# A hybrid decoder layer: order and number of GpSimd's clears before attention, and products of 128 columns in place of 256

## The chip, the cores and the metric

The kernel runs on one core of a Trainium2 chip. The time is that of one execution on the device, in microseconds; the kernel before takes 741.02 us (median of 3 runs, 740.92 to 741.1). The core has a matrix engine (TensorE, PE in the profile), a vector engine (VectorE, DVE), a scalar engine (ScalarE, ACT), GpSimd (POOL), and SyncE (SP), which here only issues DMA transfers.

## The reference

One decoder layer over 512 tokens of 1024 channels. Two causal attention branches of 8 heads (64 channels a head) work on the same modulated input; their outputs are projected, gated, merged, and followed by a layer norm and a gated MLP with a short causal convolution. The part that the change touches is attention:

```python
logits = einsum('bhqd,bhkd->bhqk', q, k) * ATTN_SCALE + c[..., None] - c[:, :, None, :]
p = softmax(where(kpos <= qpos, logits, -inf))            # forgetting branch
y_fox = einsum('bhqk,bhkd->bhqd', p, v)

z = einsum('bhqd,bhkd->bhqk', q, k) * ATTN_SCALE           # stick-breaking branch
rest = reverse_cumsum(where(kpos < qpos, log_sigmoid(-z), 0)) (exclusive)
a = where(kpos < qpos, exp(log_sigmoid(z) + rest), 0)
y_sb = einsum('bhqk,bhkd->bhqd', a, v)
```

`c` is the running sum of log forget gates. Both branches are causal: a query block of 128 tokens needs only the key blocks up to its own.

## The kernel before, in words

Matrix products are done in a 32-bit type that TensorE reads with fewer mantissa bits (fp32r; the profile prints operands of products as f32). To keep precision, an operand is split into a high and a low part, `hi_of` on ACT (line 91) and `lo_of` on DVE (line 94), and a product is the sum of three: high by high, high by low, low by high. Projections go through `mm3` (lines 132 to 134), 512 columns each.

First comes a stage that loads the modulation weights and does the first projections while loading (line 336). Attention follows. Its work is a list of projections (`stream`, through `proj` and `vgroup`) that fills TensorE between the steps of 16 heads: 8 of the stick-breaking branch (branch 1) first, then 8 of the forgetting branch (branch 0). The head loop calls for each head `stage_a`, `stage_b` and `stage_c`, with `fill(n)` for so many projection products between them. The order of SyncE's DMA issues is that of the source; on the other engines the framework's planner orders the instructions, and may move one ahead of another whose inputs it expects later. So TensorE's instructions do not always lie in the order of the source.

`stage_a` computes the scores of the four query blocks i, in the order 0, 2, 1, 3, by two products each: line 512 with `m1` (key, high part above and once more below), line 513 with `m2`, whose upper 64 rows hold the key's low part (line 455) and whose lower 64 rows are zero in the stick-breaking branch; in the forgetting branch four of them carry the decay terms (`decay_rows`: four rows of ones, then rows of `chi` by GpSimd's DMAs). Block i needs (i + 1) x 128 columns of keys, but no product is narrower than 256 (line 510): block 0 computes 128 columns that nobody reads. The scores lie in three PSUM banks (`OFS`); block 0 has the first 128 columns of bank 0, and block 2 the other 384. In branch 1, ACT takes two sigmoids of each bank (lines 535, 536), DVE scans (540) and GpSimd multiplies (541).

`m2` and its partner on the query side, `s2`, are views of four rotating tiles each (`m2t`, `s2t`). GpSimd clears their lower halves once, before attention: each query tile by three pieces (64 rows to 0, four to 1, two to -1, lines 375 to 377), then each key tile by one (line 379). In branch 1 `s2` is not used; `s1` stands in for it.

`stage_b` transposes the weights block by block on TensorE (line 561, plain fp32 with the identity) and splits them. The third group holds block (3,3), then (2,2) and (2,3), in a tile `ptc` of 512 columns from column 128 on; columns 0 to 127 of `ptc` are zero, cleared once by GpSimd (line 371).

`stage_c` multiplies values by the transposed weights (line 579), for each of the high and low parts one product per key block j, in the order 0 to 3. Key block 3 touches only query block 3, that is 128 columns, but its product takes 256, of which the first 128 are the zeros of `ptc` (`AVL`).

Of the kernel before, what the change touches and what calls it, by code (L numbers as in the profile page):

```python
# [9 lines left out]
F32R = mybir.dt.float32r  # L10
# [6 lines left out]
P = 128  # L17
# [34 lines left out]
def layer_kernel(ctx: ExitStack, tc: tile.TileContext, out, xT, x, c8, wa0, wa1, bcol, w1, wct, wv, bf,  # L52
# [3 lines left out]
    V, S, G, PE = nc.vector, nc.scalar, nc.gpsimd, nc.tensor  # L56
# [16 lines left out]
    def nm(s):  # L73
        cnt[0] += 1
        return f"{s}_{cnt[0]}"

    def bank():
        return pp.tile([P, 512], F32, name=nm("ps"), tag="ps")
# [8 lines left out]
    def fl(ap):  # L87
        return ap.bitcast(F32)

    def hi_of(o, i, scale=1.0):  # L90
        S.activation(o, i, AF.Copy, scale=scale)

    def lo_of(o, i, hi):
        state["read"] = V.tensor_tensor(o, i, fl(hi), ALU.subtract)  # L94
        return state["read"]
# [32 lines left out]
    def z(dt, s, shape=(P, 512)):  # L128
        return zp.tile(list(shape), dt, name=nm(s), tag="z", bufs=NZ)
# [14 lines left out]
    def weights(i, ahead=AHEAD):  # L144
        while state["load"] < min(len(items), i + depth[0]):
            it = items[state["load"]]
            if it[2] == 512:
                late = state.get("late")
                it[3] = late.tile([P, 512], F32, name=nm("rl"), tag="rl", bufs=4) if late else z(F32, "rs")
            else:  # L150
                it[3] = stg.tile([P, 1024], F32, name=nm("raw"), tag="raw", bufs=LOADS)
            c = 0
            for src in it[0] if isinstance(it[0], list) else [it[0]]:
                w = src.shape[-1]
                d = nc.sync.dma_start(it[3][:, c : c + w], src)
                c += w
                if depth[0] < LOADS and state["load"] >= depth[0]:
                    if reads[state["load"] - depth[0]] is None:
                        release()
                    paced(d, reads[state["load"] - depth[0]])  # L160
            if len(it) > 5:
                G.dma_start(it[3], it[5], accum_op=ALU.add)  # L162
            state["load"] += 1
            while state["proc"] <= state["load"] - depth[0]:
                process()
        while state["proc"] < min(len(items), i + 1 + ahead):
            process()
        return items[i][4]
# [42 lines left out]
    for k in range(KT):  # L211
        o = grp[k // 4][:, k % 4 * P : (k % 4 + 1) * P]
# [151 lines left out]
    att = st2.enter_context(tc.tile_pool(name="att", bufs=1, reuse_waits="tile"))  # L364

    OFS = ((0, 0), (2, 0), (0, 128), (1, 0))
    SEG = (((0, 128), (128, 512)), ((0, 512),), ((0, 256),))
    ptc = [[att.tile([P, 512], F32R, name=f"ptc{i}{e}", tag=f"ptc{i}{e}") for e in range(2)] for i in range(2)]
    for e in ptc:
        for t in e:  # L370
            G.memset(fl(t[:, 0:128]), 0.0)
    s2t = [att.tile([P, 512], F32R, name=f"s2_{i}", tag=f"s2_{i}") for i in range(4)]
    m2t = [att.tile([P, 512], F32R, name=f"m2_{i}", tag=f"m2_{i}") for i in range(4)]
    for t in s2t:
        G.memset(fl(t[64:128, :]), 0.0)
        G.memset(fl(t[64:68, :]), 1.0)
        G.memset(fl(t[64:66, :]), -1.0)
    for t in m2t:
        G.memset(fl(t[64:128, :]), 0.0)
    chi = att.tile([NH, 2, 512], F32R, name="chi", tag="chi")  # L380


# [22 lines left out]
    def decay_rows(h):  # L405
        n = slot_free(idx(0, h))
        if h < 4:
            G.memset(fl(m2t[n][64:68, :]), 1.0)
        G.dma_start(s2t[n][66:68, :], chi[h : h + 1, :, :])
        G.dma_start(m2t[n][64:66, :], chi[h : h + 1, :, :])  # L410
# [9 lines left out]
    def idx(br, h):  # L420
        return h if br == 1 else NH + h
# [43 lines left out]
    def v_part(br, h, j):  # L465
        o = ((h // 2) % 2) * 256 + (h % 2) * P
        return vt[(br, j, h // 4)][:, o : o + P]
# [36 lines left out]
    def stage_a(br, h):  # L504
        d = hd[(br, h)]
        bk = [bank(), bank(), bank()]

        def scores(i):
            b, o = OFS[i]
            w = max(256, (i + 1) * P)  # L510
            tb = slice(i * P, (i + 1) * P)
            PE.matmul(bk[b][:, o : o + w], d["s1"][:, tb], d["m1"][:, 0:w], start=True, stop=False)  # L512
            PE.matmul(bk[b][:, o : o + w], d["s2"][:, tb], d["m2"][:, 0:w], start=False, stop=True)  # L513

        for i in (0, 2, 1, 3):
            scores(i)
        pt = [z(F32, "pt"), z(F32, "pt"), z(F32, "pt")]
        if br == 0:
            sm = att.tile([P, 12], F32, name=nm("sm"), tag="sm", bufs=3)
            for i in (0, 2, 1, 3):  # L520
                b, o = OFS[i]
                c = slice(o, o + (i + 1) * P)
                n, m = pt[b][:, c], mska[:, (3 - i) * P : 512]
                V.tensor_tensor_reduce(n, bk[b][:, c], m, -1.0, -NEG, ALU.add, ALU.min, sm[:, i : i + 1])
                S.activation(n, n, AF.Exp, scale=-1.0, bias=sm[:, i : i + 1], accum_out=sm[:, 4 + i : 5 + i])
            V.reciprocal(sm[:, 8:12], sm[:, 4:8])
            for i in (0, 2, 1, 3):
                b, o = OFS[i]
                c = slice(o, o + (i + 1) * P)
                V.tensor_scalar_mul(pt[b][:, c], pt[b][:, c], sm[:, 8 + i : 9 + i])  # L530
        else:
            for b in (0, 2, 1):
                w = SEG[b][-1][1]
                om = z(F32, "om")
                S.activation(om[:, 0:w], bk[b][:, 0:w], AF.Sigmoid, scale=-1.0)  # L535
                d["last"] = S.activation(pt[b][:, 0:w], bk[b][:, 0:w], AF.Sigmoid)
                G.memset(pt[b][:, SEG[b][0][1] - 1 : w : 384], 0.0)
                for s, e in SEG[b]:
                    d0 = om[:, s + 1 : e][:, ::-1]
                    V.tensor_tensor_scan(d0, d0, dg[:, 513 - (e - s) : 512][:, ::-1], 0.0, ALU.mult, ALU.max)  # L540
                    G.tensor_tensor(pt[b][:, s : e - 1], pt[b][:, s : e - 1], om[:, s + 1 : e], ALU.mult)  # L541
        d["pt"] = pt
        scored.add(idx(br, h))
        if br == 0 and h + 4 < NH:
            decay_rows(h + 4)
        if br == 1 and h >= 4 and gated:
            decay_rows(h - 4)
# [3 lines left out]
    def stage_b(br, h):  # L551
        d = hd[(br, h)]
        pt = d["pt"]
        n = h % 2
        d["ph"], d["pl"] = [], []
        for e, lst in enumerate(TRL):
            bk = bank()
            w = len(lst) * P
            for q, (j, i) in enumerate(lst):
                b, o = OFS[i]  # L560
                PE.transpose(bk[:, q * P : (q + 1) * P], pt[b][:, o + j * P : o + (j + 1) * P], ident)  # L561
            if e < 2:
                ph, pl, o = z(F32R, "ph"), z(F32R, "pl"), 0
            else:
                (ph, pl), o = ptc[n], 128
            hi_of(ph[:, o : o + w], bk[:, 0:w])
            lo_of(pl[:, o : o + w], bk[:, 0:w], ph[:, o : o + w])
            d["ph"].append(ph)
            d["pl"].append(pl)

    AVL = ((0, 0, 0, 0, 512), (1, 1, 0, 128, 384), (2, 2, 256, 256, 256), (3, 2, 0, 256, 256))
    yf, yh, yl = {}, {}, {}

    def stage_c(br, h):
        d = hd.pop((br, h))
        ps = bank()
        for a, src in enumerate((d["ph"], d["pl"])):
            for j, e, so, to, w in AVL:
                PE.matmul(ps[:, to : to + w], v_part(br, h, j), src[e][:, so : so + w], start=a == 0 and j == 0, stop=a == 1 and j == 3)  # L579
# [227 lines left out]
    stage_a(1, 1)  # L807
    fill(48)
    stage_b(1, 0)
    fill(48)  # L810
    heads = [(br, 2 * p + e) for br, p in seq for e in range(2)]
# [182 lines left out]
    for n in range(2 * FT):  # L994
# [7 lines left out]
        if n in (23, 27):  # L1002
            t = t13[(23, 27).index(n)][:, 0:512]
# [5 lines left out]
        if n in (28, 31, 32, 35):  # L1009
            k = (28, 31, 32, 35).index(n)  # L1010
            w = wdp[FP - 1][:, k * 512 : (k + 1) * 512]
# [115 lines left out]
    for n in range(2 * FT):  # L1127
# [27 lines left out]
        t = z(F32, "cv")  # L1155
# [131 lines left out]
    for n, k in enumerate(wi):  # L1287
        w = weights(k)
        for a, p in enumerate(range(2 * n, min(FP - LATE, 2 * n + 2))):
            t = ops[p][3]  # L1290
# [5 lines left out]
    for i in range(2):  # L1296
        pieces = [(1, 0, 512)] if i == 0 else [(1, 0, 256), (1, 256, 512)]
        for n, (e, c0, c1) in enumerate(pieces):
            ps = bank()[:, 0 : c1 - c0] if i else W1[0]
            for q in range(LATE):  # L1300
                t = ops[FP - LATE + q][3]
# [72 lines left out]
```

## Time and profile before

| | |
|---|---|
| median of 3 runs | 741.02 us |
| the profiled execution | 741.73 us, of which 740.0 us is the span of the trace |
| PE busy | 728.0 us (98%) |
| DVE busy | 600.6 us (81%) |
| ACT busy | 389.4 us (53%) |
| POOL busy | 86.5 us (12%) |
| attention's heads in the trace | scores from 54.5 to 267 us, value products from 97 to 289 us |

Instructions are named by engine, line, and tiles, output first (`ps<-m,s`: into PSUM from the key and query tiles). In a timeline the first number is the start in microseconds from the span's start, the second how long the group of merged instructions lasts, then x and their count; in brackets stand the idle time before it and who ended it. PEld is TensorE's weight load, which overlaps products. Products are pipelined: one lasts longer than the time to the next one's start, so a cost on PE is read from start to start, and the shown end is modelled. In a waits view a row gives waiter, releaser, total wait, times and the longest.

### The profile page before, as it was taken

The numbers are of one execution on the slowest core, as the hardware profiler recorded it, in microseconds if no ns is written. First come the engines' busy times: TensorE is split into PE (matmuls) and PEld (weight loads), VectorE is DVE, ScalarE is ACT, GpSimd is POOL, SyncE is SP. The second block draws the span as 40 slices with busy tenths as digits, with TensorE's granted clock in tenths as the row PEclk, the third lists the DMA queues.
The fourth block names the chain that finished last, engine by engine and source line by source line (L and its number), as shares of the span: only waits on it lengthen the run. The fifth ranks groups of instructions, "written<-read, shape, count | busy, mean of one in ns | idle before, by whom it ended". The sixth has DMA issues, their size and how long they took to land.

```text
span 740.0 us, 9862 instructions
## 1 busy us (share of the span) xinstructions
PE 728.0 (98%) x3449; PEld 608.4 (82%) x3449; DVE 600.6 (81%) x1049; ACT 389.4 (53%) x679; POOL 86.5 (12%) x150
## 2 busy tenths in 40 slices
PE   9999999999999999999999999999999999999995
PEld 6888878888888888888889888888888788887885
DVE  6878689878798895884588989977887787679996
ACT  4566466685986664542065554444453544347550
POOL 1036133334010000000000001000011011000010
PEclk9999999999999999999999999999999999999999
DMA  9942643522431332642074678578799777646733
GB/s 342 405 166 81 229 145 142 176 81 88 171 108 65 115 114 89 223 150 85 1 250 135 217 226 253 173 229 228 212 345 252 200 239 206 207 157 227 228 86 85
DMA packets 45346, 131.96 MB, mean 178 GB/s; under 512 B 6152, under 2 KB 6672, under 8 KB 45296
## 3 DMA queue, kind: packets, MB, share of 16 engines
q1 hardware_dynamic: 38032, 112.61, 44.6%
q0 software_dynamic: 4224, 10.30, 7.0%
q10 hardware_dynamic: 3040, 8.42, 3.1%
q8 instruction: 27, 0.44, 0.3%
q14 instruction: 23, 0.19, 0.1%
HBM read 118.39 MB, written 12.85 MB: 177 GB/s over the span
## 4 chain that ended last, share of the span: by engine, by line
PE 90%; DVE 4%; DMA 2%; ACT 1%; issue 1%; POOL 1%; ACTq 0%; SPq 0%; DVEq 0%; POOLq 0%
PE ps L132 18%; PE ps L133 18%; PE ps L134 18%; PE ps L336 5%; PE ps L1104 5%; PE ps L1105 5%; PE ps L1106 5%; PE ps L579 3%; PE ps L561 2%; PE ps L903 2%; PE ps L901 2%; PE ps L902 2%; PE ps L513 1%; PE ps L512 1%; PE ps L487 1%; PE ps L488 1%
## 5 line engine op out<-in xcount | busy, mean ns | idle before, releaser
L196 ACT ACTIVATE wh<-raw 128x1024 fp32r<-128x1024 f32 (+1 forms) x105 | 109.1, 1041 | 106.6 <-PE ps L133 45.1
L94 DVE TENSOR_TENSOR wl<-raw,wh 128x1024 fp32r<-128x1024 f32 (+2 forms) x114 | 135.4, 1190 | 35.4 <-ACT wh L196 34.4
L133 PE MATMUL ps<-u2l,wh 128*128 128x512 f32 (+1 forms) x376 | 141.2, 376 | 0.0
L134 PE MATMUL ps<-u2h,wl 128*128 128x512 f32 (+1 forms) x376 | 141.1, 376 | 0.0
L132 PE MATMUL ps<-u2h,wh 128*128 128x512 f32 (+1 forms) x376 | 141.0, 376 | 0.0
L134 PEld LDWEIGHTS ps<-u2h,wl 128*128 128x128 f32 x376 | 70.8, 188 | 12.9
L133 PEld LDWEIGHTS ps<-u2l,wh 128*128 128x128 f32 x376 | 70.8, 188 | 12.7
L132 PEld LDWEIGHTS ps<-u2h,wh 128*128 128x128 f32 x376 | 70.6, 188 | 12.8
L132 PE MATMUL ps<-uh,wh 128*128 128x512 f32 x200 | 78.9, 395 | 0.0
L133 PE MATMUL ps<-ul,wh 128*128 128x512 f32 x200 | 78.1, 391 | 0.0
L134 PE MATMUL ps<-uh,wl 128*128 128x512 f32 x200 | 78.1, 390 | 0.0
L1157 ACT ACTIVATE cv<-ps,cw 128x512 f32<-128x512 f32 x44 | 34.0, 773 | 49.7 <-PE ps L134 42.2
L1158 DVE SCALAR_TENSOR_TENSOR cv<-ps,cw,cv 128x511 f32<-128x511 f32 x44 | 32.8, 746 | 24.4 <-ACT cv L1157 24.3
L134 PEld LDWEIGHTS ps<-uh,wl 128*128 128x128 f32 x200 | 37.5, 188 | 8.3 <-DVE wl L94 0.2
L132 PEld LDWEIGHTS ps<-uh,wh 128*128 128x128 f32 x200 | 37.6, 188 | 7.4
L133 PEld LDWEIGHTS ps<-ul,wh 128*128 128x128 f32 x200 | 37.6, 188 | 7.3
L219 DVE SCALAR_TENSOR_TENSOR raw<-raw,cbc 128x1024 f32<-128x1024 f32 x32 | 40.1, 1254 | 0.0
L162 POOL DMA_DIRECT2D raw<-in_wdp x10 | 8.9, 890 | 246.2 <-DMA raw<-in_wdp 228.4
L541 POOL TENSOR_TENSOR pt<-pt,om 128x127 f32<-128x127 f32 (+3 forms) x32 | 36.5, 1151 | 1.7 <-DVE om L540 1.2
L540 DVE TENSOR_TENSOR_SCAN om<-om,dg 128x127 f32<-128x127 f32 (+3 forms) x32 | 30.2, 1005 | 4.9 <-ACT om L535 4.8
L1159 DVE SCALAR_TENSOR_TENSOR cv<-ps,cw,cv 128x510 f32<-128x510 f32 x44 | 32.7, 744 | 0.4
L1165 ACT ACTIVATE cv<-cv 128x512 f32<-128x512 f32 x22 | 13.9, 631 | 31.6 <-DVE cv L1159 31.6
(232 smaller groups left out, 1562.7 us busy)
## 6 DMA issues: line engine op xcount, KB each, us to landing
raw<-in_wup SPq DMA_DIRECT2D x44, 512.0 KB, 4.7
raw<-in_wa SPq DMA_DIRECT2D x32, 512.0 KB, 3.7
raw<-in_wct SPq DMA_DIRECT2D x25, 512.0 KB, 4.4
raw<-in_wdp SPq DMA_DIRECT2D x20, 512.0 KB, 5.3
wa<-in_wa SPq DMA_DIRECT2D x15, 512.0 KB, 7.4
raw<-in_wdp SPq DMA_DIRECT2D x22, 256.0 KB, 4.8
raw<-t SPq DMA_DIRECT2D x22, 256.0 KB, 4.3
raw<-in_wdp POOLq DMA_DIRECT2D x10, 512.0 KB, 7.6
```

Of the source, the lines that this page charges most:

```text
L94: state["read"] = V.tensor_tensor(o, i, fl(hi), ALU.subtract)
L132: PE.matmul(ps, wh, ah, start=first, stop=False)
L133: PE.matmul(ps, wh, al, start=False, stop=False)
L134: return PE.matmul(ps, wl, ah, start=False, stop=last)
L196: state["hi"] = S.activation(h[:, 0:cols], r[:, 0:cols], AF.Copy)
L219: state["read"] = V.scalar_tensor_tensor(wt[:, c], wt[:, c], 1.0, cbc[:, c] if by is None else by, ALU.mult, ALU.mult, accum_out=o)
L336: PE.matmul(grp[g], w, u, start=j == 0 and n == 0, stop=j == KT - 1 and n == (1 if g == 7 else 2))
L541: G.tensor_tensor(pt[b][:, s : e - 1], pt[b][:, s : e - 1], om[:, s + 1 : e], ALU.mult)
L1104: PE.matmul(ps, ah, bh, start=first, stop=False, skip_group_check=onto)
L1105: PE.matmul(ps, ah, bl, start=False, stop=False, skip_group_check=onto)
L1106: return PE.matmul(ps, al, bh, start=False, stop=last, skip_group_check=onto)
L1157: S.activation(t, ps, AF.Identity, bias=cw[:, n, 3:4], scale=cw[:, n, 2:3])
```

## The change

The `ptc` tiles become 384 columns wide and are no longer cleared; block (3,3) starts at column 0. GpSimd clears the four key tiles first; each query tile is then set by one clear of its 64 lower rows to -1, in place of three. (Its rows of decay are written over as before, and what stands in its remaining rows meets zeros of the key tile.) The scores of query block 0 are computed over 128 columns, and the value products of key block 3 over 128. Nothing is moved among the other instructions of the source.

```diff
-    ptc = [[att.tile([P, 512], F32R, name=f"ptc{i}{e}", tag=f"ptc{i}{e}") for e in range(2)] for i in range(2)]
-    for e in ptc:
-        for t in e:
-            G.memset(fl(t[:, 0:128]), 0.0)
+    ptc = [[att.tile([P, 384], F32R, name=f"ptc{i}{e}", tag=f"ptc{i}{e}") for e in range(2)] for i in range(2)]
     s2t = [att.tile([P, 512], F32R, name=f"s2_{i}", tag=f"s2_{i}") for i in range(4)]
     m2t = [att.tile([P, 512], F32R, name=f"m2_{i}", tag=f"m2_{i}") for i in range(4)]
-    for t in s2t:
-        G.memset(fl(t[64:128, :]), 0.0)
-        G.memset(fl(t[64:68, :]), 1.0)
-        G.memset(fl(t[64:66, :]), -1.0)
     for t in m2t:
         G.memset(fl(t[64:128, :]), 0.0)
+    for t in s2t:
+        G.memset(fl(t[64:128, :]), -1.0)
...
-            w = max(256, (i + 1) * P)
+            w = (i + 1) * P
...
             else:
-                (ph, pl), o = ptc[n], 128
+                (ph, pl), o = ptc[n], 0
...
-    AVL = ((0, 0, 0, 0, 512), (1, 1, 0, 128, 384), (2, 2, 256, 256, 256), (3, 2, 0, 256, 256))
+    AVL = ((0, 0, 0, 0, 512), (1, 1, 0, 128, 384), (2, 2, 128, 256, 256), (3, 2, 0, 384, 128))
```

## The prediction, made before the changed kernel was run

> **What bounds the kernel now.** I read the page first, then TensorE's waits, then the stages that the diff touches in the timelines of PE, POOL, ACT and DVE, and last the chain of waits through the two places where PE stood.
>
> ```profile
> PE 728.0 (98%) x3449; PEld 608.4 (82%) x3449; DVE 600.6 (81%) x1049; ACT 389.4 (53%) x679; POOL 86.5 (12%) x150
> PE ps L579 <- DVE vv L94: 1.6, 1, 1.6
> PE ps L513 <- POOL m L379: 0.6, 1, 0.6
> 100.00:290.00 190.00, 190.00 (x973) 162.22 (x972) 159.52 (x296) 131.64 (x253) 35.23 (x60) 1.00 0.35 120
> ```
>
> The first row is the page's busy times, the next two come from PE's waits, the last is the stage table (sum, then PE, PEld, DVE, ACT, POOL, clock, DMA share, GB/s). PE is the bound: from 100 to 290 us, where nearly all of the edited products lie, it never stands, while DVE has 30 us of room and ACT 58. So a step saved on PE there should reach the end, and one added surely does. Before 100 us PE stands twice, and one of the two is a wait for a GpSimd clear of a key tile (line 379). The profiled execution took 741.73 us: 740.0 of span and 1.73 around it. That is 0.71 above the median of the runs, 741.02. I sum changes against the profile and take them from the median.
>
> **Part 1: the order of the clears.** GpSimd's timeline, and PE's at the first head's scores:
>
> ```profile
> 49.46 0.63 POOL L371 MEMSET ptc<- 128x128 f32 x4 [45.76 <-ACT s L91]
> 54.77 0.98 POOL L377 MEMSET s<- 2x512 f32 x2
> 55.70 1.90 POOL L379 MEMSET m<- 64x512 f32 x4
> 54.54 0.63 PE L512 MATMUL ps<-m,s 128*128 128x256 f32 x3
> 55.01 0.40 PE L132 MATMUL ps<-uh,wh 128*128 128x512 f32 x1
> 55.24 0.39 PE L133 MATMUL ps<-ul,wh 128*128 128x512 f32 x1
> 56.27 0.38 PE L513 MATMUL ps<-m,s 128*128 128x256 f32 x1 [0.64 <-POOL m L379]
> 57.19 0.39 PE L134 MATMUL ps<-uh,wl 128*128 128x512 f32 x1
> ```
>
> POOL starts at 49.46, clears four `ptc` tiles and twelve pieces of the query tiles, and comes to the key tiles only at 55.70. Three of the four L512 products have gone by then; L513 reads the key tile and waits to 56.27. The change drops the `ptc` clears and eight of the twelve query clears, and puts the keys first. I take it that the first clear still begins at 49.46, since it takes over memory of the stage before, whichever tile it is. Then four key clears end near 49.46 + 1.90 = 51.4 and four query clears near 53.3. GpSimd's next work is at 58, and nobody wants the query tiles (used in the forgetting branch alone) until much later, so their move costs nothing; without that cover it would be four clears, 1.9 us of POOL. No DMA is moved.
>
> What else must be ready for L513 is the lower half of the product's key operand, written by DVE; the second head's scores show a set without a stall:
>
> ```profile
> 51.84 1.39 DVE L94 TENSOR_TENSOR m<-ps,m 64x512 fp32r<-64x512 f32 x2 [1.05 <-ACT m L91]
> 60.60 0.39 PE L134 MATMUL ps<-uh,wl 128*128 128x512 f32 x1
> 60.83 0.28 PE L512 MATMUL ps<-m,s 128*128 128x256 f32 x1
> 60.94 0.28 PE L513 MATMUL ps<-m,s 128*128 128x256 f32 x1
> 61.06 0.34 PE L512 MATMUL ps<-m,s 128*128 128x384 f32 x1
> 61.24 0.34 PE L513 MATMUL ps<-m,s 128*128 128x384 f32 x1
> 62.10 0.39 PE L132 MATMUL ps<-uh,wh 128*128 128x512 f32 x1
> ```
>
> DVE is done at 53.23, ahead of 54.54. A clean set takes 62.10 - 60.83 = 1.27 us. The first one took 57.19 - 54.54 = 2.65, less two projection products (L132, L133, about 0.46 together): 2.19. PE gains 0.92 there: the wait and the shuffled order.
>
> Whether that reaches the end depends on the second wait, at 99.45, where the slack of PE would be spent. So I followed what leads to it.
>
> ```profile
> 57.04 0.60 ACT L535 ACTIVATE om<-ps 128x512 f32<-128x512 f32 x1 [3.67 <-PE ps L513]
> 59.49 2.13 ACT L624 ACTIVATE sg<-ps 128x512 f32<-128x512 f32 x4
> 61.40 1.25 ACT L91 ACTIVATE s<-ps 64x512 fp32r<-64x512 f32 x2
> 71.91 4.26 DMA raw<-in_wv
> 90.31 3.66 DVE om L540 x4
> 99.07 0.34 DVE vv L94
> 97.52 0.28 PE L579 MATMUL ps<-ptc,vv 128*128 128x256 f32 x1
> 99.45 0.39 PE L579 MATMUL ps<-ptc,vv 128*128 128x256 f32 x1 [1.65 <-DVE vv L94]
> 100.08 0.40 PE L579 MATMUL ps<-ptc,vv 128*128 128x256 f32 x2
> 100.32 0.39 PE L132 MATMUL ps<-uh,wh 128*128 128x512 f32 x1
> ```
>
> The first three are ACT's timeline, the next three pieces of the chain of waits, the rest PE's timeline. The chain to 99.45 goes back through DVE, a value-weight load and ACT to the same first scores: ACT idles 3.67 us and is let go at 57.04 by L513, then works without a gap to 62.65. With the keys clear, the fourth product of the set starts 61.24 - 60.83 = 0.41 after the first and lasts 0.34, so ACT starts at 54.54 + 0.75 = 55.29, 1.7 earlier. That lead isn't all kept: the two `s` copies at 61.40 need the projection that ends at 60.60 + 0.39 = 60.99, which moves by PE's own 0.92, to 60.07. So ACT's gain from there is 61.40 - 60.07 = 1.3 us, and I let the chain carry it: the loads on it are issued as buffers come free, and these follow ACT and DVE. PE comes to the wait 0.92 earlier, the chain ends 1.3 earlier, so the wait shrinks from 1.65 to about 1.3 and stays; up to 99.45 the chain sets the time, and part 1 is worth **1.3 us**. Bounds: 0 (a link of the chain doesn't move and the wait swallows it) and 1.7 (ACT's whole lead carried).
>
> **Part 2: narrower products.** In each of 16 heads two score products (L512, L513 of block 0) and two value products (L579 of key block 3, high and low part) go from 256 to 128 columns: 64. Those ahead of 99.45 run inside the slack of the wait: the first three heads' scores (6) and the value product that itself waited. 57 count. Each keeps its own weight load. What a 256-column product costs from start to start is above: 61.06 - 60.83 over two is 0.115, 100.32 - 100.08 over two is 0.12; I take 0.1175. No fp32r product of 128 columns is in the trace, so I bound it by rows:
>
> ```profile
> 108.67 0.39 PE L133 MATMUL ps<-ul,wh 128*128 128x512 f32 x1
> 108.90 0.39 PE L134 MATMUL ps<-uh,wl 128*128 128x512 f32 x1
> 109.13 1.25 PE L561 MATMUL ps<-ident,pt 128*128 128x128 f32 x10
> L561 PE MATMUL ps<-ident,pt 128*128 128x128 f32 x160 | 20.3, 273 | 0.0
> 56.27 0.19 PEld L513 LDWEIGHTS ps<-m,s 128*128 128x128 f32 x1 [1.07 <-POOL m L379]
> 56.38 0.19 PEld L512 LDWEIGHTS ps<-m,s 128*128 128x128 f32 x1
> 2.59 3.78 PE L213 MATMUL ps<-c8s,ident 8*128 8x128 f32 x16
> 6.30 3.59 PE L208 MATMUL ps<-warm 128*128 128x512 bf16 x8
> ```
>
> Low end: 512 columns step 0.23 and 256 step 0.1175, so 128 fewer columns take off about 0.055: 0.063. Middle: ten transposes of 128 columns, each with its own weights, take 1.25, so they step (1.25 - 0.273)/9 = 0.109. The stalled L513 says why: its weight load and the product were released together at 56.27, the next load came 0.11 later, and that product shows 0.38 where its like shows 0.28. A load so takes about 0.105, and the next can't begin before the product ahead has taken its own. A product behind another with other weights thus can't step by less than a load, however few columns it streams. High end: the eight plain-fp32 products of line 213, two records each, step (3.78 - 0.42)/15 = 0.224 a record; the clock was lower there (512 bf16 columns step about 0.42, later 0.23), so at the later speed some 0.24 for a 128-column product.
>
> I take 0.109, the row nearest in kind: 128 columns with a fresh load each. 57 x (0.1175 - 0.109) = **0.5 us**. The low end gives 57 x 0.055 = 3.1, the high end costs 57 x 0.1225 = 7.0. The narrower score also leaves columns 128 to 255 to the third block's own first product, and the value product no longer reads zeros; neither adds an instruction.
>
> The row puts the step at 0.109. The Trainium skill (TensorE: Matmul & The Clock Gate, section Back-to-back issue gap) gives about 81 ns for a sustained stream of load and product pairs at 128 columns, and 56 ns for a product alone. By the 81 ns the sum would be 57 x 0.0365 = 2.1 in place of 0.5, an estimate of 737.6 us. No fp32r run here shows it, and the transposes speak against it.
>
> **Sum.** 1.3 + 0.5 = 1.8 us: 741.73 becomes about 739.9 in a profiled execution, and 741.02 becomes **739.2 us**, 0.24% less.
>
> **The rivals.**
> (a) The load doesn't bound fp32r products and a narrow one steps by its columns: 1.3 + 3.1 = 4.4, 736.6 us. For it: 512, 384 and 256 columns lie on one line (0.23, 0.18, 0.1175) with no floor in sight. Against it: the transposes, and the load of 0.105 at 56.27.
> (b) The wait at 99.45 takes the place of the one removed: the chain's loads or DVE's scans come no sooner, PE arrives 0.92 earlier and stands 0.92 longer. Only part 2 is left: 740.5 us. For it: the chain runs through DMA and a busy DVE (four scans of 3.66 us), and PE's instructions already lie in another order than the source's, so the planner may lay the new ones out differently there. Against it: every link starts from ACT's late start at 57.04.
> (c) Slower: a product of under 256 columns in this type goes through the array in four passes, as the plain fp32 ones of line 213 do. The place is all 64 narrow products, the price 0.1225 each on the path; the change is slower from a step of about 0.14 (1.3 / 57 above 0.1175). 57 x 0.1225 - 1.3 = 5.7: 746.7 us. For it: line 213 shows that a product on 32-bit data can take more than one pass, and no fp32r product under 256 columns runs here that would exclude it. Against it: from 512 to 256 columns the step shrinks in proportion, with nothing that depends on the width.
>
> **How the numbers follow.** The forecast has 0.50, (a) 0.13, (b) 0.22, (c) 0.15. A measurement of this kernel can tell about 0.2% (1.5 us) from no change: faster is under 739.5, slower over 742.5. The forecast's own range is 738.4 to 740.2 (part 1 from 0.5 to 1.7, part 2 from 0.3 to 0.9), of which some seven tenths is faster: 0.35 + 0.13 makes 0.49 with a little of (b); the rest of the forecast and (b) make 0.36 for the same; (c) is the 0.15. The range takes in (a) and (b) with some room for (b) losing another 0.7, and leaves (c) out: 736.4 to 741.2.
>
> **What would show it.** PE's waits: no row L513 <- POOL; the first head's eight scores in about 1.25 us. GpSimd: four key clears from 49.5 on, no `ptc`. ACT's first L535 near 55.3. The row L579 <- DVE vv still there with about 1.3 us, ending near 98.1; at 1.65 or more with the end at 99.4, (b) is right. The step behind a 128-column L512 or L579 near 0.109; 0.063 is (a), 0.2 or more is (c). PE busy without a gap from 100 us on; a new row of PE waiting for DVE or ACT there would undo part 2, and a start of the first key clear later than 54 would undo part 1.

## The result, and the profile after

The changed kernel takes 738.08 us (median of 6 runs, 737.67 to 738.47) against 741.24 for the kernel before (6 runs beside it, 740.92 to 741.92): a ratio of 0.9957 with a 95% interval of 0.9947 to 0.9967, 3.2 us less. Forecast were 1.8 us less, 739.2 us, in a range from 736.4 to 741.2. The time lies in the range, but below the 738.4 to 740.2 that the forecast gave itself.

The profiled execution took 737.75 us, 736.0 of them the span. These are, of the kernel after, the page's busy times, TensorE's waits (one row is all that is left) and two rows of the stage table (sum, PE, PEld, DVE, ACT, POOL, clock, DMA share, GB/s):

```profile
PE 726.9 (99%) x3449; PEld 607.6 (83%) x3449; DVE 598.9 (81%) x1049; ACT 389.9 (53%) x679; POOL 85.0 (12%) x138
PE ps L208 <- DVE warm L106: 1.2, 1, 1.2
48.00:100.00 52.00, 52.00 (x250) 43.69 (x249) 42.29 (x58) 32.55 (x61) 16.10 (x21) 1.00 0.41 141
100.00:290.00 190.00, 190.00 (x972) 161.49 (x972) 157.96 (x295) 130.90 (x252) 37.49 (x60) 1.00 0.34 118
```

Both of PE's waits before 100 us are gone, the one on the key clear and the one on the last value block. In the stage from 48 to 100 us PE was busy for 49.71 us of 52 before, and is now for all of it. The row of before:

```profile
48.00:100.00 52.00, 49.71 (x236) 41.17 (x235) 40.17 (x53) 29.72 (x58) 23.57 (x41) 1.00 0.38 132
```

GpSimd's timeline, after:

```profile
39.31 1.90 POOL L372 MEMSET m<- 64x512 f32 x4 [35.60 <-DVE modc L225]
44.23 1.91 POOL L374 MEMSET s<- 64x512 f32 x4 [3.02 <-DVE wa L219]
```

The key clears don't begin at 49.5 but at 39.3, ten microseconds earlier than forecast. PE's timeline, after: the first head's scores and the first head's values.

```profile
54.70 0.22 PE L507 MATMUL ps<-m,s 128*128 128x128 f32 x1
54.76 0.28 PE L508 MATMUL ps<-m,s 128*128 128x128 f32 x1
54.87 0.39 PE L507 MATMUL ps<-m,s 128*128 128x384 f32 x1
55.10 0.34 PE L508 MATMUL ps<-m,s 128*128 128x384 f32 x1
55.97 0.40 PE L132 MATMUL ps<-uh,wh 128*128 128x512 f32 x1
58.50 0.39 PE L134 MATMUL ps<-uh,wl 128*128 128x512 f32 x1
59.86 0.39 PE L134 MATMUL ps<-uh,wl 128*128 128x512 f32 x1
96.25 0.56 PE L574 MATMUL ps<-ph,vv 128*128 128x512 f32 x2
96.65 0.34 PE L574 MATMUL ps<-ptc,vv 128*128 128x256 f32 x2
97.30 0.34 PE L574 MATMUL ps<-ptc,vv 128*128 128x256 f32 x2
97.47 0.45 PE L132 MATMUL ps<-uh,wh 128*128 128x512 f32 x1
97.76 0.40 PE L133 MATMUL ps<-ul,wh 128*128 128x512 f32 x1
```

The scores take 55.97 - 54.70 = 1.27 us, as the undisturbed second set did before. The values run through: 97.47 - 96.25 = 1.22 us. The narrow products do step quickly (54.76 - 54.70 = 0.06), but what follows is slower: the 384-column product at 54.87 takes 0.23 to the next one where its like took 0.18 before (61.06 to 61.24), and the L132 at 97.47 takes 0.29 in place of 0.23.

Where the time went is best read within a trace, from start to start, because the first score product starts anywhere from 54.54 to 56.01 us in the profiles of these kernels. I take two stretches: stretch A from the first score product to the L133 behind the first value set, stretch B from there to the L133 behind the last value set. Before, they are 100.55 - 54.54 = 46.01 and 289.20 - 100.55 = 188.65; after, 97.76 - 54.70 = 43.06 and 286.19 - 97.76 = 188.43. A gives 2.95 us and B 0.22, in sum 3.17, about the difference of the medians. A holds part 1 of the prediction, B nearly all of part 2. PE's timeline, before (the start of the first value set and the end of B) and after (the end of B):

```profile
97.13 0.56 PE L579 MATMUL ps<-ph,vv 128*128 128x512 f32 x2
289.20 0.40 PE L133 MATMUL ps<-yl,wh 128*128 128x512 f32 x1
```
```profile
286.19 0.40 PE L133 MATMUL ps<-yl,wh 128*128 128x512 f32 x1
```

A's gain lies where PE stood. The first scores took 0.92 less (1.27 in place of 2.19), and the first value set 1.97 less (1.22 in place of 100.32 - 97.13 = 3.19): 2.89 of 2.95.

Why did A give 2.95 and not 1.3? ACT's and SyncE's timelines, after:

```profile
55.47 0.60 ACT L530 ACTIVATE om<-ps 128x512 f32<-128x512 f32 x1 [1.94 <-PE ps L508]
59.83 1.24 ACT L91 ACTIVATE s<-ps 64x512 fp32r<-64x512 f32 x2
60.97 1.05 ACT L196 ACTIVATE wh<-raw 128x1024 fp32r<-128x1024 f32 x1
62.05 0.60 ACT L530 ACTIVATE om<-ps 128x512 f32<-128x512 f32 x1
69.44 0.38 SPq L155 DMA_DIRECT2D raw<-in_wv  x1
```

and the answering rows of before:

```profile
62.67 0.60 ACT L535 ACTIVATE om<-ps 128x512 f32<-128x512 f32 x1
65.12 2.17 ACT L196 ACTIVATE wh<-raw 128x1024 fp32r<-128x1024 f32 x2
71.91 0.38 SPq L155 DMA_DIRECT2D raw<-in_wv  x1
```

Counted from the first score product, ACT starts at 0.77 us in place of 2.50, that is 1.73 earlier, as forecast (1.7). But at 60.97 one split of weights (line 196) now stands ahead of the second head's sigmoids; before, it came behind them (65.12). DVE's half of it (`wl`) moved too, from behind DVE's scans (67.79) to ahead of them (62.53). So L219, the step of DVE for which SyncE's next loads wait, comes sooner: at 67.35 in place of 69.30. The load of the value weights (`in_wv`), a link of the chain to the second wait, is issued 14.74 us after the first score in place of 17.37: 2.63 earlier in place of 1.3.

My theory after the result (A): the gain is the two waits; the second one vanished because the chain to it starts earlier and, beyond that, because the planner moved this split. Against it stood (B), that the narrow products carry the gain, and (C), that the order on ACT has no part.

### The profile page after: what moved, and what is told of

Its sections match the earlier page's. It is cut to its first block, busy times and chain, and to the rows that moved or that the text cites. A ratio compares the mean times of both kernels' runs of the same rounds, so it can differ in the third digit from the quotient of the medians.

```text
span 736.0 us, 9853 instructions
## 1 busy us (share of the span) xinstructions
PE 726.9 (99%) x3449; PEld 607.6 (83%) x3449; DVE 598.9 (81%) x1049; ACT 389.9 (53%) x679; POOL 85.0 (12%) x138
## 4 chain that ended last, share of the span: by engine, by line
PE 99%; DVE 1%; issue 0%; DVEq 0%
PE ps L132 19%; PE ps L134 19%; PE ps L133 19%; PE ps L336 6%; PE ps L1099 5%; PE ps L1101 5%; PE ps L1100 5%; PE ps L574 3%; PE ps L556 2%; PE ps L482 2%; PE ps L484 2%; PE ps L483 2%; PE ps L897 2%; PE ps L898 2%; PE ps L896 2%; PE ps L508 1%
## 5 line engine op out<-in xcount | busy, mean ns | idle before, releaser
L133 PE MATMUL ps<-u2l,wh 128*128 128x512 f32 (+1 forms) x376 | 141.2, 376 | 0.0
L132 PE MATMUL ps<-u2h,wh 128*128 128x512 f32 (+1 forms) x376 | 141.0, 376 | 0.0
L133 PEld LDWEIGHTS ps<-u2l,wh 128*128 128x128 f32 x376 | 70.8, 188 | 12.8
L132 PEld LDWEIGHTS ps<-u2h,wh 128*128 128x128 f32 x376 | 70.6, 188 | 12.7
L132 PE MATMUL ps<-uh,wh 128*128 128x512 f32 x200 | 79.5, 397 | 0.0
L133 PE MATMUL ps<-ul,wh 128*128 128x512 f32 x200 | 77.9, 390 | 0.0
L133 PEld LDWEIGHTS ps<-ul,wh 128*128 128x128 f32 x200 | 37.6, 188 | 7.4
L132 PEld LDWEIGHTS ps<-uh,wh 128*128 128x128 f32 x200 | 37.5, 188 | 7.4
L536 POOL TENSOR_TENSOR pt<-pt,om 128x127 f32<-128x127 f32 (+3 forms) x32 | 39.5, 1244 | 1.1 <-DVE om L535 1.0
L219 DVE SCALAR_TENSOR_TENSOR raw<-raw,cbc 128x1024 f32<-128x1024 f32 x32 | 39.6, 1238 | 0.0
L535 DVE TENSOR_TENSOR_SCAN om<-om,dg 128x127 f32<-128x127 f32 (+3 forms) x32 | 27.3, 913 | 3.6 <-ACT om L530 3.6
```

What stands on the lines that cost most here:

```text
L132: PE.matmul(ps, wh, ah, start=first, stop=False)
L133: PE.matmul(ps, wh, al, start=False, stop=False)
L219: state["read"] = V.scalar_tensor_tensor(wt[:, c], wt[:, c], 1.0, cbc[:, c] if by is None else by, ALU.mult, ALU.mult, accum_out=o)
```

## The experiments

Each was timed 5 to 11 times, beside the kernel before on the same chip; stretches are from each profile, as above, and good to about 0.01.

| kernel | us | ratio to before (95%) | A | B |
|---|---|---|---|---|
| before | 741.24 (740.99 to 741.43 beside the others) | | 46.01 | 188.65 |
| the change | 738.08 | 0.9957 (0.9947 to 0.9967) | 43.06 | 188.43 |
| e1: clears alone | 738.14 | 0.9955 (0.9941 to 0.9968) | 43.06 | 188.66 |
| e2: narrow products alone | 740.84 | 0.9995 (0.9987 to 1.0004) | 45.96 | 188.43 |
| e6: the change, split held back | 739.09 | 0.9976 (0.9966 to 0.9985) | 44.31 | 188.45 |
| e7: before, split put ahead | 740.26 | 0.9987 (0.9979 to 0.9996) | 45.26 | 188.63 |
| e9: before, `ptc` cleared last | 739.66 | 0.9979 (0.9970 to 0.9987) | 44.68 | 188.63 |
| e3: before, keys first, `ptc` last | 738.32 | 0.9958 (0.9945 to 0.9972) | 43.06 | 188.65 |
| e4: the change, block 1's scores split | 741.26 | 1.0001 (0.9992 to 1.0010) | 43.64 | 190.95 |
| e5: the change, last value product 64 wide | 737.57; 737.61 | 0.9954 (0.9942 to 0.9967); 0.9952 (0.9939 to 0.9964) | 43.06 | 188.44 |
| the change again, beside e4 and e5 | 738.46; 738.08 | 0.9961 (0.9949 to 0.9974); 0.9954 (0.9942 to 0.9967) | 43.05; 43.06 | 188.44; 188.43 |

**The two parts apart (e1, e2).** e1 has the new clears with products of 256 columns (the `ptc` clears kept, at the end):

```diff
-    for e in ptc:
-        for t in e:
-            G.memset(fl(t[:, 0:128]), 0.0)
...
-    for t in s2t:
-        G.memset(fl(t[64:128, :]), 0.0)
-        G.memset(fl(t[64:68, :]), 1.0)
-        G.memset(fl(t[64:66, :]), -1.0)
     for t in m2t:
         G.memset(fl(t[64:128, :]), 0.0)
+    for t in s2t:
+        G.memset(fl(t[64:128, :]), -1.0)
+    for e in ptc:
+        for t in e:
+            G.memset(fl(t[:, 0:128]), 0.0)
```

> The clears alone: key tiles first, each query tile by one clear, the zeros of ptc last; products stay at 256 columns. Theory A (the gain comes from the two waits before 100 us: 0.9 us at the first scores, the rest because the chain to the second wait starts earlier and one weight split moved ahead of the second head's sigmoids on ACT): nearly all of the gain is here, about 2.9 us, 738.3 us, with neither wait in PE's waits. Rival B (narrow products carry most of the gain): about 1.3 us or less, near 740.

Measured: 738.14 us, A 43.06. e2 has the narrow products with the clears of before:

```diff
-            w = max(256, (i + 1) * P)
+            w = (i + 1) * P
...
-    AVL = (..., (2, 2, 256, 256, 256), (3, 2, 0, 256, 256))
+    AVL = (..., (2, 2, 256, 256, 256), (3, 2, 128, 384, 128))
```

> The 128-column products alone, clears as before. Theory A with a load as the floor of a product's step: the narrow product steps by 57 ns, but the next one gives it back; 64 products save 4 to 7 ns each, 0.3 us, 740.9 us, and both waits stay. Rival B (each narrow product saves its columns, 55 ns): 3.1 us less, 738.1 us.

Measured: 740.84 us, no difference that can be told; B is 0.22 shorter, A 0.05. PE's waits in e2:

```profile
PE ps L579 <- DVE vv L94: 1.5, 1, 1.5
PE ps L513 <- POOL m L379: 0.9, 1, 0.9
```

Rival B falls: the clears are the whole measurable gain, and the narrow products give 0.2 us.

**The split on ACT (e6, e7).** e6 is the changed kernel, where that split must be issued behind the second head's last sigmoid; the scores on TensorE keep the changed kernel's order:

```diff
-        state["hi"] = S.activation(h[:, 0:cols], r[:, 0:cols], AF.Copy)
+        hold = state.pop("hold", None)
+        with tc.issue_after(hold.ins) if hold else ExitStack():
+            state["hi"] = S.activation(h[:, 0:cols], r[:, 0:cols], AF.Copy)
...
     stage_a(1, 1)
+    state["hold"] = hd[(1, 1)]["last"]
```

> The changed kernel, with the one ACT split of the value weights that the planner had put ahead of the second head's sigmoids held behind them, as before. Theory A: the load that its buffer frees is issued some 0.9 us later, and the wait for the last value block comes back at about 0.9 us: 739.0 us, 0.9 above the changed kernel. Rival C (the planner's order had no part; the earlier start of the chain alone removed the wait): the time of the changed kernel, 738.1 us, no wait.

Measured: 739.09 us (the profiled execution, at 740.87, was the longest of nine; what it has more lies outside A and B), and the wait is back at the value product. PE's, ACT's and SyncE's timelines, e6:

```profile
55.55 0.22 PE L509 MATMUL ps<-m,s 128*128 128x128 f32 x1
97.50 0.28 PE L576 MATMUL ps<-ptc,vv 128*128 128x256 f32 x1
98.76 0.33 PE L576 MATMUL ps<-ptc,vv 128*128 128x128 f32 x1 [0.98 <-DVE vv L94]
56.32 0.60 ACT L532 ACTIVATE om<-ps 128x512 f32<-128x512 f32 x1 [1.93 <-PE ps L510]
71.19 0.38 SPq L155 DMA_DIRECT2D raw<-in_wv  x1
```

A is 1.25 longer than in the changed kernel and 1.70 shorter than before. ACT starts 0.77 after the first score, as in the changed kernel; the load is issued at 15.64, 1.73 earlier than before and 0.90 later than in the changed kernel. So with the split in its old place, the chain carries ACT's whole lead of 1.73, and the split adds 0.90 to the load.

ACT's order differs in this one instruction, but DVE's differs too. SyncE's next loads wait for L219. DVE's timelines, the changed kernel and then e6, whose line 221 is the same step:

```profile
75.96 1.22 DVE L219 SCALAR_TENSOR_TENSOR raw<-raw,cbc 128x1024 f32<-128x1024 f32 x1
77.22 1.16 DVE L94 TENSOR_TENSOR pl<-ps,ph 128x512 fp32r<-128x512 f32 x2
```
```profile
77.88 1.16 DVE L94 TENSOR_TENSOR pl<-ps,ph 128x512 fp32r<-128x512 f32 x2
79.41 1.22 DVE L221 SCALAR_TENSOR_TENSOR raw<-raw,cbc 128x1024 f32<-128x1024 f32 x1
```

In the changed kernel L219 stands ahead of the splits `pl` of the transposed weights, in e6 behind them, as before; the next load of the chain (`in_wct`) is issued 2.60 later in e6. So the 1.25 belongs to the split and to what the planner moved on DVE with it; e6 doesn't part the two. e7 does the reverse to the kernel before: its second head's first sigmoid must come behind the split, and nothing else is edited.

```diff
+        om = state.pop("om", None)
+        if om:
+            d = mybir.DependencyInfo(mybir.DependencyClass.NoSync, mybir.DependencyReason.DATA)
+            tc.add_manual_dep(om.ins, state["hi"].ins.name, d, reason="order")
...
     stage_a(1, 1)
+    state["om"] = hd[(1, 1)]["first"]
```

> The kernel before, with that one split put ahead of the second head's first sigmoid, and no other edit. Theory A: the wait on the clear of the key tile stays (0.6 us), the second wait shrinks from 1.65 to about 0.75: 740.3 us. Rival C: nothing, 741.2 us.

Measured: 740.26 us. PE's timeline, e7:

```profile
56.70 0.38 PE L517 MATMUL ps<-m,s 128*128 128x256 f32 x1 [0.67 <-POOL m L383]
99.11 0.39 PE L585 MATMUL ps<-ptc,vv 128*128 128x256 f32 x1 [1.02 <-DVE vv L94]
```

The key wait stays, the second one shrinks from 1.65 to 1.02, and A is 0.75 shorter; L219 stays behind `pl`. Rival C falls: the place of this split is worth 0.75 us without the earlier start, and the split with DVE's new order is worth 1.25 on top of it.

**Which of the clears held the keys (e9, e3).** I had taken the first clear to start at 49.5 whichever tile it is. It started at 39.3. e9 is the kernel before with the four `ptc` clears moved behind all others; the twelve query clears stay ahead of the keys.

```diff
-    for e in ptc:
-        for t in e:
-            G.memset(fl(t[:, 0:128]), 0.0)
...
     for t in m2t:
         G.memset(fl(t[64:128, :]), 0.0)
+    for e in ptc:
+        for t in e:
+            G.memset(fl(t[:, 0:128]), 0.0)
```

> The kernel before with one edit: the four clears of ptc come after all the others; the twelve query clears still stand ahead of the key clears, and the products are as before. Theory D (the keys came late because the ptc clear, at the head of GpSimd's queue, waited until 49.5 us for memory that the stage before still used; the number of clears and the keys' place behind the queries are not the cause): the queries start near 44.5 us, the keys near 50, the wait on the key tile is gone. ACT's order is that of before, so the second wait stays at about 1 us: 739.3 us. Rival E (it is the keys' place or the twelve clears): the keys come at 55 us or later, the wait stays, 741 us.

Measured: 739.66 us. GpSimd's, PE's and ACT's timelines, e9:

```profile
44.01 0.98 POOL L372 MEMSET s<- 64x512 f32 x2 [40.30 <-DVE modc L225]
49.56 1.91 POOL L376 MEMSET m<- 64x512 f32 x4
51.52 0.64 POOL L379 MEMSET ptc<- 128x128 f32 x4
54.84 0.63 PE L512 MATMUL ps<-m,s 128*128 128x256 f32 x3
96.77 0.28 PE L579 MATMUL ps<-ptc,vv 128*128 128x256 f32 x1
98.42 0.39 PE L579 MATMUL ps<-ptc,vv 128*128 128x256 f32 x1 [1.37 <-DVE vv L94]
55.98 0.60 ACT L535 ACTIVATE om<-ps 128x512 f32<-128x512 f32 x1 [2.31 <-PE ps L513]
```

The wait on the key clear is gone, though twelve query clears still come first: what had held the keys was `ptc` at the head of GpSimd's queue, waiting until 49.46 for a split on ACT (L91, named in its row). In e1, with the queue empty ahead of it, the `ptc` clear still waits 3.59 us for ACT's L91, until 49.98. That it waits there because its memory was in use by the stage before is my reading of the source; no run shows it. The second wait stays, at 1.37, for ACT's order is that of before. A gives 1.33 us. This is less than in e6, because the first scores keep their shuffled order (three L512 first): ACT starts 1.14 after the first score, a lead of 1.36. Here too A gains what ACT gains. e3 puts the keys first, then the same twelve query clears, then `ptc`:

> The kernel before with the order of the clears alone changed: keys, then all twelve query clears, then ptc. Products stay at 256 columns. Theory A/D (what counts is that the keys don't stand behind ptc, and that the planner then puts the split ahead; the eight dropped clears don't count): as with the clears of the change, 738.3 us, no PE wait before 100 us. Rival F (the dropped clears matter, through GpSimd's time): above 739.

Measured: 738.32 us, A 43.06, as with four query clears. So the eight dropped clears have no part in the time. With the keys first the planner puts the split ahead (e1, e3, and the change itself); with the keys behind the queries it doesn't (e9). Why its order turns on that, no run shows.

**What a narrow product costs (e4, e5).** e4 computes block 1's scores by two products of 128 columns for each of 256: as many columns, 32 more products.

```diff
-            PE.matmul(bk[b][:, o : o + w], d["s1"][:, tb], d["m1"][:, 0:w], start=True, stop=False)
-            PE.matmul(bk[b][:, o : o + w], d["s2"][:, tb], d["m2"][:, 0:w], start=False, stop=True)
+            for c in ((0, P), (P, 2 * P)) if i == 1 else ((0, w),):
+                k = slice(*c)
+                q = slice(o + c[0], o + c[1])
+                PE.matmul(bk[b][:, q], d["s1"][:, tb], d["m1"][:, k], start=True, stop=False)
+                PE.matmul(bk[b][:, q], d["s2"][:, tb], d["m2"][:, k], start=False, stop=True)
```

> The changed kernel with the scores of query block 1 as two products of 128 columns for each one of 256: 32 products more, the same columns in all. Theory A (no product behind another costs less than its weight load, about 0.109 us): two of 256 take 0.235 us, four of 128 take 0.436, so 0.2 us more for each of 16 heads, 3.2 us, 741.3 us. Rival B (a product costs its columns and some 9 ns): 0.3 us more, 738.4 us.

The changed kernel ran beside it:

> The changed kernel once more, on the chip of the three below: 738.1 us, so that they can be set against it.

Measured: 741.26 us, against 738.46 for the changed kernel: 2.8 us more. PE's timeline, e4:

```profile
61.39 0.22 PE L510 MATMUL ps<-m,s 128*128 128x128 f32 x1
61.45 0.27 PE L511 MATMUL ps<-m,s 128*128 128x128 f32 x1
61.56 0.27 PE L510 MATMUL ps<-m,s 128*128 128x128 f32 x1
61.67 0.28 PE L511 MATMUL ps<-m,s 128*128 128x128 f32 x1
61.78 0.45 PE L510 MATMUL ps<-m,s 128*128 128x512 f32 x1
62.06 0.39 PE L511 MATMUL ps<-m,s 128*128 128x512 f32 x1
```

Only the first narrow product steps by 0.06; the next three step by 0.11, and the 512-column one behind takes 0.28. The weight loads start every 0.11 us through this row, at 61.39, 61.50, 61.61, 61.72 and 61.83, whatever the products' starts show; so the floor is theirs as far as the trace tells. No run has a narrow product without a load of its own. In B the 13 heads cost 190.95 - 188.43 = 2.52 us, 0.19 a head. e5 makes the last value product 64 columns wide in place of 128 (the values of the last block for the last 64 queries are left out).

> The changed kernel with the value product of key block 3 over 64 columns in place of 128; it leaves out the last block's values for the last 64 queries. Theory A (the load is the floor): no change, 738.1 us. Rival B (columns): 32 products by 27 ns, 0.9 us less, 737.2 us.

Measured: 737.57 us against 738.46 beside it, which would have been rival B's 0.9; but B was 188.44, not shorter. So I ran both again:

> The changed kernel on the same chip, for comparison with the next: 738.2 us.

> The kernel with the last value product over 64 columns again (it leaves out the last block's values for the last 64 queries), because its median was 0.9 us below the changed kernel's while its trace shows only some 0.15 us less up to 570 us. If the load is the floor: within 0.3 us of the changed kernel beside it. If columns count: 0.9 us less again, in the part from 97 to 290 us.

Measured: 737.61 against 738.08, with B again 188.44 against 188.43. Halving the columns of 32 products changes nothing where they run: it shows as a product that steps by 0.03 and a next one that takes that back. The medians' differences of 0.9 and 0.5 don't come from A or B, and each time the single runs of the two kernels overlap (737.16 to 738.80 against 737.72 to 738.82, and 737.38 to 738.26 against 737.37 to 738.28). Behind B, where nothing was edited, the profiles of one and the same kernel differ by up to a microsecond (441.4 to 442.5 us from the end of B to the last product in three profiles of the changed kernel; 441.7 and 441.8 in those of e5). So I count them as scatter between executions; nothing shows another cause.

## Why the prediction was right, and where it fell short

**PE is the bound and stands twice before 100 us; what is saved there reaches the end.** Right: A and B together make 3.17 us, and the medians differ by 3.16.

**The first wait.** Right in the wait and in the size of what PE loses there (a clean set of 1.27 us in place of 2.19). The step that the first clear still begins at 49.46 was wrong: the key clears wait for a DVE product of the first stage (modc, L225) and began at 39.31, while `ptc` waits for ACT until 49.46. It didn't matter for the time, since 51.4 would have been early enough; it did for the cause, which is `ptc` at the head of the queue and not the number of clears (e9, e3).

**The chain to the second wait: 1.3 us, "so the wait shrinks from 1.65 to about 1.3 and stays".** This is the step that failed, and the term that was mis-sized: A gave 2.95. The mechanism, a chain that starts with ACT's first sigmoid, was right. Two sizes were not.

The first is the cut from 1.7 to 1.3. It rested on the two `s` copies of ACT needing a projection that ends just ahead of the second head's scores. In the changed kernel these copies start at 59.83, ahead of the last product there (59.86), so they don't need it. By the source, a projection takes 24 products, and 12 of this one run before the first scores; the other 12 end with the product at 58.50. ACT comes to the copies without idling, before and after, so nothing trims its lead. Where the split keeps its place, A gains ACT's lead whole: 1.70 for a lead of 1.73 (e6), 1.33 for 1.36 (e9). The upper bound of 1.7 was the right sum.

The second is the planner. With the key clears first it issues one weight split ahead of the second head's sigmoids, and L219 on DVE ahead of `pl`. The load comes forward by another 0.90 us and PE runs through; that is worth the other 1.25 (e6). I had named the planner only in rival (b), as a risk, and had no row for it.

That the time still lies in the range is in part luck: its low end made room for rival (a), and the 3.2 us came another way.

**The narrow products: 0.109 a step, 0.5 us.** The floor was right, the sum a little too large: B gives 0.22 for 56 products, 4 ns each in place of 8.5. A narrow product with its own load costs no less with half the columns (e5), and four of 128 columns cost more than two of 256 (e4: 0.19 a head, where 0.2 follows from 0.109 against 0.1175). That a single step of 0.06 stands in the trace, which was to show rival (a), doesn't make (a) right: the time comes back at the next product. By the Trainium skill's 81 ns for such a stream (TensorE: Matmul & The Clock Gate, section Back-to-back issue gap) part 2 would have been 2.1 us, an estimate; the narrow products of e4 in a row step by 0.11, and B gave 0.22. One reading behind the high end stands on less than it seems: the granted clock of the profile is 1.00 from 2.5 to 10 us as well, so the lower clock there rests on the slower steps alone.

**The rivals.** (a) would have shortened B by 3.1: it shrank by 0.22. (b) would have left A where it was: it lost 2.95. (c), four passes, would have shown 0.2 or more from a narrow product's start to the next and a longer B: neither is there.

## What to carry to other kernels

Before narrowing products, look at what their weight loads allow: here, where each product brings its own weights, one of 128 columns costs nearly as much as one of 256 (0.11 against 0.1175 us), and the sum over a group of products tells it, not the step of one. When a wait goes away, compare the order of the instructions on the other engines as well: here the place of four clears let the planner move a split on ACT and more behind it on DVE, and that was 1.25 of 3.2 us. And here an instruction that waited at the head of GpSimd's queue held everything behind it: what is wanted first belongs first, and above all not behind something that can't start.

## What the runs showed that was not expected

The step behind one product's recorded start doesn't give its cost. Behind a narrow product the next one starts early in the trace and then takes longer by the same amount: 0.06 and then 0.23 for 384 columns, in place of 0.12 and 0.18.

GpSimd's clears of 512 columns cost the same whether they cover 64, 4 or 2 partitions (0.98 to 0.99 us for two of each kind in the kernel before). Three clears of parts thus cost three times one clear of the whole, though here nobody waits for them any more.

DVE's scans over 511 columns grew shorter and GpSimd's products over 127 longer, though neither was edited. Groups by line, before and after:

```profile
L540 DVE TENSOR_TENSOR_SCAN om<-om,dg 128x511 f32<-128x511 f32 x8 | 14.7, 1836 | 0.0
L541 POOL TENSOR_TENSOR pt<-pt,om 128x127 f32<-128x127 f32 x8 | 6.1, 760 | 1.1 <-DVE om L540 0.7 <-issue 0.3
```
```profile
L535 DVE TENSOR_TENSOR_SCAN om<-om,dg 128x511 f32<-128x511 f32 x8 | 12.4, 1544 | 0.0
L536 POOL TENSOR_TENSOR pt<-pt,om 128x127 f32<-128x127 f32 x8 | 8.7, 1093 | 1.1 <-DVE om L535 1.0
```

The two work at the same time on the same scores, so which of them yields may depend on how they meet; that was not tried. Both parts of the change have a share: all of these scans take 32.1 us before, 31.3 in e1, 30.1 in e2 and 29.2 after, and GpSimd's products 36.9, 37.8, 38.5 and 39.7. From 100 us on neither holds PE, which never stands there.
